# One hybrid decoder layer on one core: the first part's input loaded in one go, and the sample rows finished before the dense tiles' last norms

## The chip, the cores and the metric

One core of a Trainium2 chip runs the whole kernel. The metric is the device time of one execution in microseconds (us); lower is better. The core has a matrix engine (TensorE, PE in the profile, its weight loads PEld), a vector engine (VectorE, DVE), a scalar engine (ScalarE, ACT), GpSimd (POOL) and SyncE (SP), which here only issues transfers. Each engine takes its own instructions strictly in program order; they wait for each other by semaphores. [...]

## The reference

One layer of a decoder for a prompt of 1024 tokens and a sample of 8 x 4 tokens, all of width 1024 and in float32:

```python
h = rms_norm(x, norm_mix);  z = h @ w_in            # 28 column chunks of 128
A = dilated sliding-window attention (8 heads x 64) # q, k, v: chunks 0..11
B = gated linear recurrence (4 heads x 128)         # q, f, i, g: chunks 12..27
x += concat([rms_norm(A), gated B]) @ w_out
x += cross_attention(rms_norm(x), memory)           # 256 memory tokens
x += peer_ffn(rms_norm(x))                          # each token: 8 heads x 16 of 16384 experts
y = rms_norm(x, norm_final)
# peer_ffn, per token: e = chosen expert numbers, g = softmax of their scores
#   a = gelu(sum_d x[d] * peer_u[e, d]);   y = sum_e g * a * peer_v[e]
```

## The kernel before

The prompt is worked in three parts of tokens, `PARTS = ((0,1,2), (3,4,8), (5,6,7))`, in tiles of 128; "tile" 8 is the 32 sample rows, which ride along with the first part through the projection `z` and with the second from there on. Everything is float32 made of two fp32r halves (`hi`, `lo`), so each product is three matmuls (lines 201 to 203): weights hi times x hi, weights hi times x lo, weights lo times x hi, for each of eight blocks `c` of 128 input columns, in the order of `c`.

**The start.** `head()` of the first part loads the tokens twice: as rows (`in_x`, tiles tagged `P`, two buffers, then a Square with an accumulated sum on ScalarE, line 326) and transposed (`in_xT`, eight column blocks, tiles `ht`, two buffers). From the sums it makes 1/rms (line 210, on GpSimd), spreads it over the partitions by TensorE (line 217) into `bc`, and `norm_T` (lines 226 to 232) then takes each block: multiply with gain and `bc` (line 230, VectorE), copy to `hi` (line 169, ScalarE), difference to `lo` (line 170, VectorE). The first projection chunk can run its block `c` when `zhi` and `zlo` of it are there. Weights come as `raw` (two buffers), are split into `wz` (three buffers), used, and written to memory (`wd`) for the later parts. Before `head()` the program loads constants: `ident`, `par`, `bias_p`, `lmask`, `misc`, `iota`, `sum4`.

**The middle.** Attention, recurrence, cross attention and the choice of experts of the three parts are interleaved generators.

**The end.** Of the nine tiles, five (`DENSE`, tiles 0 to 4) are done by `dense()`: all 128 groups of 128 experts are streamed through TensorE (`a` = x times u, gelu, times gate, then `y`/`yr` = w times v); three tiles stay in PSUM (`y0`..`y5`), two are added to `ys` by VectorE from the one bank `yr`. `u` tiles have 5 buffers, `v` tiles 11. The other four tiles (8, 7, 6, 5, in this order) are done by `gather_tile()`: for each of up to 128 experts of a token GpSimd fetches one row per token (`row`, 7 buffers, line 1183), VectorE multiplies and sums (line 1190 for peer_u, line 1201 for peer_v, into `ha`). The two streams run side by side: TensorE works on dense, GpSimd and VectorE on the gather with VectorE's share of dense between. Behind each tile stands `final_norm` (lines 1144 to 1153): Square on ScalarE, a small VectorE step, a power on GpSimd (line 1149), the load of the final gain `gfin` spread over the rows (line 1151), a VectorE multiply, the store. The sample rows, whose gather tile was the first of the four and waits in memory as `accd`, are finished by `finish_sample` (lines 1207 to 1216): two matmuls sum four groups of rows, then `final_norm`.

The order on each engine is made by the framework's list scheduler, which follows a time line of its own; code that stands earlier comes first among what is ready. It also hands out the buffers of a tag. SP's transfers use eight completion slots in turn: a transfer is issued only after the one eight before it has landed.

Of the kernel before, what the change touches and what calls it, by code (L numbers as in the profile page):

```python
# [20 lines left out]
D = 1024  # L21
# [8 lines left out]
def col(p, n):  # L30
    return p[:, n : n + 1]
# [33 lines left out]
def _body(tc, nc, ctx, A, O):  # L65
# [43 lines left out]
    par = T(cst, [128, 64], F32, "par")  # L109
    SP.dma_start(par, A["par"])  # L110
    G_MIX, G_CR, G_FFN, G_MEM, BETA, GNB, LBL = 0, 8, 16, 24, 32, 36, 40
    bias_p = T(wk, [128, 1024], F32, "biasp")
    SP.dma_start(bias_p, A["bias_p"])
    lmask = T(wk, [128, 8, 128], U8, "lmask")
    lmf = T(pk, [128, 8, 128], F32, "tw", 2)
    SP.dma_start(lmf, A["lmask"])
    V.tensor_copy(lmask, lmf)
    smask = T(cst, [32, 3, 32], U8, "smask")
    V.tensor_copy(smask, lmf[:32, :3, :32])
    misc = T(cst, [128, 64], F32, "misc")  # L120
    SP.dma_start(misc, A["misc"])
    DM_A, DM_X, SEL, BEX = misc[:, 0:8], misc[:, 8:12], misc[:, 12:28], misc[0:32, 28:36]
# [175 lines left out]
    def part(pi):  # L298
# [21 lines left out]
        def head():  # L320
            ss = T(wk, [128, 4], F32, "n_ss")
            V.memset(ss, 1.0)
            for j, (t, o, rows) in enumerate(zt):
                m = T(wk, [128, 1024], F32, "P", 2)
                SP.dma_start(m[:rows], A["x"][t * 128 : t * 128 + rows, :])
                S.activation(m[:rows], m[:rows], AF.Square, accum_out=col(ss, j)[:rows])
            bc = bcast(rstd_of(ss[:, : len(zt)], len(zt), D), zt, "m", HB)

            def x_of(c):
                t = T(wk, [128, WZ], F32, "ht", HTB)[:, :WZP]  # L330
                load_xT(t, c, WZP)
                return t

            h.extend(norm_T(x_of, WZP, G_MIX, bc, hi_lo(TAGS["Z"]), True))

# [704 lines left out]
    def dense(dv, dn, dps):  # L1040
# [66 lines left out]
        for i in range(128):  # L1107
            hist.append(nxt)
            nxt = []
            ahead = hidden(i + 1, nxt) if i < 127 else iter(())  # L1110
            kept = [(t, dh) for t in range(KEEP) for dh in range(2)]
            sums = [(t, dh) for t in range(KEEP, NDT) if i % GRP == t % GRP or i == 127 for dh in range(2)]

            def keep(n):
                for t, dh in kept[:n]:
                    product(yp[2 * t + dh], t, dh, hist[i:], i == 0, i == 127)
                del kept[:n]

            next(ahead, None)
            keep(KEEP - 1)  # L1120
            next(ahead, None)
            for t, dh in sums:
                keep(1)
                ds = slice(dh * 512, (dh + 1) * 512)
                o = T(dps, [128, 512], F32, "yr", 1 if KEEP > 2 else 2)
                product(o, t, dh, hist[done[t] :], True, True)
                V.tensor_tensor(ys[t - KEEP][:, ds], ys[t - KEEP][:, ds], o, op=ALU.add)  # L1127
                done[t] = done[t] + dh * (i + 1 - done[t])
            keep(len(kept))
            next(ahead, None)  # L1130
            yield
        for t in range(NDT):
            if t < KEEP:
                acc = T(dn, [128, D], F32, "u", 5)
                SP.dma_start(acc, x2d[DENSE[t]])
                for dh in range(2):
                    ds = slice(dh * 512, (dh + 1) * 512)
                    V.tensor_tensor(acc[:, ds], acc[:, ds], yp[2 * t + dh], op=ALU.add)
            else:
                acc = ys[t - KEEP]  # L1140
            final_norm(acc, 128, O["y_prompt"][DENSE[t] * 128 : (DENSE[t] + 1) * 128, :],
                       lambda: T(dn, [128, D], F32, "u", 5), dn)

    def final_norm(acc, rows, out, row, p):
        st = T(p, [128, 4], F32, "fst", 2)
        jk = row()
        S.activation(jk[:rows], acc, AF.Square, accum_out=col(st, 0)[:rows])
        V.tensor_scalar(col(st, 1)[:rows], col(st, 0)[:rows], 1.0 / D, EPS, op0=ALU.mult, op1=ALU.add)
        G.tensor_tensor(col(st, 2)[:rows], col(st, 1)[:rows], mhalf[:rows, 0:1], op=ALU.pow)
        gfin = row()  # L1150
        SP.dma_start(gfin[:rows], A["gfin"].to_broadcast([rows, 1024]))
        V.scalar_tensor_tensor(acc, acc, col(st, 2)[:rows], gfin[:rows], op0=ALU.mult, op1=ALU.mult)
        SP.dma_start(out, acc)

# [7 lines left out]
            return T(more, [128, D], F32, "row", MR)  # L1162
        return T(gat, [128, D], F32, "row", 2)

    def gather_tile(t):
        smp = t == 8
        nj = 32 if smp else 128
        ix = T(gat, [128, 128], U32, "ix", 2)[:, :nj]
# [33 lines left out]
        if smp:  # L1202
            SP.dma_start(accd, acc)
        else:
            final_norm(acc, 128, O["y_prompt"][t * 128 : (t + 1) * 128, :], g_row, gat)

    def finish_sample(dn, dps):
        row = lambda: T(dn, [128, D], F32, "u", 5)
        acc = row()
        SP.dma_start(acc, accd)  # L1210
# [1 line left out]
        for n in range(2):  # L1212
            p = T(dps, [128, 512], F32, "yr", 1)
            PE.matmul(p[:32], lhsT=sum4, rhs=acc[:, n * 512 : (n + 1) * 512], start=True, stop=True)
            V.tensor_copy(fin[:32, n * 512 : (n + 1) * 512], p[:32])
        final_norm(fin[:32], 32, O["y_sample"], row, dn)

    def run(weights, *gens):
        gens = [(iter(g), n) for g, n in zip(gens, weights)]
# [20 lines left out]
    def ahead(q):  # L1240
        q.head()
        q.first_a()

    ahead(p[0])
    p[0].first_h()
    run(W0, p[0].middle(lambda: ahead(p[1])), memory_kv())
    p[1].first_h()
# [6 lines left out]
    with tc.tile_pool(name="dn", bufs=1, reuse_waits="tile") as dn, \  # L1254
# [4 lines left out]
            f()  # L1259
        late.close()  # L1260
        more = ctx.enter_context(tc.tile_pool(name="more", bufs=1, side="right", reuse_waits="tile"))
        for _ in work:
            pass
        for t in [t for part in PARTS for t in sorted(part, reverse=True) if t not in DENSE]:
            gather_tile(t)
        finish_sample(dn, dps)


def _consts():
# [100 lines left out]
```

## Time and profile before

| | |
|---|---|
| median of 3 runs | 3629.08 us (3626.5 to 3631.28) |
| profiled execution: time, span | 3627.68 us, 3625.8 us |
| busy: PE, DVE, ACT, POOL | 3373.7, 2634.7, 1220.6, 1112.5 us |
| transfers | 1007.82 MB, 278 GB/s over the span |

The span is the time between the first and the last recorded instruction; the execution's own time is 1.88 us longer. Busy times of engines overlap, so they do not add up to the span. A busy matrix engine is not one at its peak, since its matmuls are pipelined.

### The profile page before, as it was taken

The page shows a single profiled execution, that of the slowest core. Times are in us where ns is not written, and L with a number is a line of the kernel's source. Part 1 is how long each engine was busy: PE and PEld are TensorE (multiplying, and loading weights), DVE is VectorE, ACT ScalarE, POOL GpSimd, SP SyncE. Part 2 cuts the span into 40 slices and gives each one's busy share as a digit, 9 for nine tenths or more (in the row PEclk, how much of TensorE's full clock was granted, in tenths as well). Part 3 has the DMA queues.
Part 4 walks back from the last instruction along what each step waited for, and adds up shares of the span by engine and source line. Part 5 has one row for each costly group of instructions (what it writes and reads, how often), then busy time and mean ns, then how long its engine had stood idle before and what let it go on. Part 6 is the DMA issues. An engine that isn't in the chain of part 4 may idle for free.

```text
span 3625.8 us, 52725 instructions
## 1 busy us (share of the span) xinstructions
PE 3373.7 (93%) x19343; PEld 2912.4 (80%) x19343; DVE 2634.7 (73%) x5868; ACT 1220.6 (34%) x2282; POOL 1112.5 (31%) x871
## 2 busy tenths in 40 slices
PE   5999999999999889887799999999999999999994
PEld 4886776677887788777788998999888898988893
DVE  4443333243885687897888878988888898888997
ACT  4544344344434443431242222222222222222221
POOL 0000000000000000021316644656566565565555
PEclk9999999999999999898999999999999999999997
DMA  7667777656655485499659988999999999999998
GB/s 243 230 226 248 239 247 240 202 181 220 210 192 201 179 293 209 150 338 344 229 169 348 341 291 286 364 351 337 340 335 351 345 333 342 337 343 332 329 328 296
DMA packets 408514, 1007.82 MB, mean 278 GB/s; under 512 B 43968, under 2 KB 168896, under 8 KB 406848
## 3 DMA queue, kind: packets, MB, share of 16 engines
q1 hardware_dynamic: 288448, 568.20, 45.6%
q0 software_dynamic: 119808, 436.26, 33.0%
q8 instruction: 152, 2.49, 0.3%
q14 instruction: 106, 0.87, 0.1%
HBM read 866.01 MB, written 138.31 MB: 277 GB/s over the span
## 4 chain that ended last, share of the span: by engine, by line
PE 71%; DVE 10%; DMA 9%; issue 4%; ACT 3%; POOL 1%; SPq 1%; POOLq 0%; DVEq 0%; ACTq 0%
PE a L201 7%; PE a L203 7%; PE a L202 7%; PE y L1098 4%; PE y L1099 4%; PE y L1100 4%; PE z L201 4%; PE z L202 3%; PE z L203 3%; PE yr L1098 3%; PE yr L1099 2%; PE yr L1100 2%; PE y L201 2%; PE y L202 2%; PE y L203 2%
## 5 line engine op out<-in xcount | busy, mean ns | idle before, releaser
L1183 POOL DMA_INDIRECT row<-in_peer_u,ix x416 | 534.6, 1285 | 635.9 <-DVE dots L1190 347.6
L1183 POOL DMA_INDIRECT row<-in_peer_v,ix x416 | 543.1, 1306 | 412.1 <-DVE ha L1201 266.5
L201 PE MATMUL a<-xh,u 128*128 128x320 f32 x2048 | 636.8, 311 | 21.2 <-ACT w L1088 18.0
L203 PE MATMUL a<-xh,u 128*128 128x320 f32 x2048 | 634.5, 310 | 0.7 <-DVE u L170 0.7
L202 PE MATMUL a<-xl,u 128*128 128x320 f32 x2048 | 634.1, 310 | 0.0
L1201 DVE SCALAR_TENSOR_TENSOR ha<-row,dots,ha 128x1024 f32<-128x1024 f32 x416 | 533.0, 1281 | 22.2 <-DMA row<-in_peer_v,ix 17.8
L1190 DVE CUSTOM_DVE_ANT_0 row<-row,ha 128x1024 f32<-128x1024 f32 x416 | 497.9, 1221 | 39.5 <-DMA row<-in_peer_u,ix 39.5
L210 POOL TENSOR_TENSOR rs_r<-rs_m,mhalf 128x3 f32<-128x3 f32 (+2 forms) x25 | 23.4, 944 | 1369.7 <-DVE rs_m L208 1250.2
L1088 ACT ACTIVATE w<-a 128x320 f32<-128x320 f32 x256 | 111.6, 436 | 937.3 <-PE a L203 917.1
L201 PEld LDWEIGHTS a<-xh,u 128*128 128x128 f32 x2048 | 385.6, 188 | 40.5 <-ACT w L1088 25.8
L202 PEld LDWEIGHTS a<-xl,u 128*128 128x128 f32 x2048 | 385.7, 188 | 8.8
L203 PEld LDWEIGHTS a<-xh,u 128*128 128x128 f32 x2048 | 385.5, 188 | 2.8 <-DVE u L170 1.0
L201 PE MATMUL z<-zhi,wz 128*128 128x384 f32 (+2 forms) x928 | 330.4, 356 | 43.0 <-DMA wz<-wd_w_pq 16.2
L202 PE MATMUL z<-zlo,wz 128*128 128x384 f32 (+2 forms) x928 | 316.8, 341 | 3.4 <-DVE zlo L170 1.9
L203 PE MATMUL z<-zhi,wz 128*128 128x384 f32 (+2 forms) x928 | 314.0, 338 | 0.0
L1099 PE MATMUL y<-v,w 128*128 128x512 f32 x768 | 294.6, 392 | 0.0
L1098 PE MATMUL y<-v,w 128*128 128x512 f32 x768 | 269.6, 393 | 12.6 <-ACT v L169 11.2
L1100 PE MATMUL y<-v,w 128*128 128x512 f32 x768 | 264.5, 391 | 1.3 <-DVE w L170 1.2
L201 PEld LDWEIGHTS z<-zhi,wz 128*128 128x128 f32 x928 | 181.0, 195 | 87.3 <-issue 21.7
L1098 PE MATMUL yr<-v,w 128*128 128x512 f32 x512 | 201.8, 394 | 13.5 <-DVE ys L1127 11.7
L169 ACT CAST w<-w 128x320 fp32r<-128x320 f32 x256 | 117.8, 460 | 259.0 <-DVE w L1090 258.5
L1100 PE MATMUL yr<-v,w 128*128 128x512 f32 x512 | 199.9, 390 | 0.7 <-DVE w L170 0.7
(470 smaller groups left out, 6685.2 us busy)
## 6 DMA issues: line engine op xcount, KB each, us to landing
u<-in_uT SPq DMA_DIRECT2D x128, 512.0 KB, 7.0
v<-in_peer_v SPq DMA_DIRECT2D x128, 512.0 KB, 7.6
wz<-wd_w_in SPq DMA_DIRECT2D x112, 512.0 KB, 4.3
gt<-gtall SPq DMA_DIRECT2D x124, 320.0 KB, 10.8
wd_w_in<-wz SPq DMA_DIRECT2D x56, 512.0 KB, 3.2
gtall<-sg SPq DMA_DIRECT2D x34, 512.0 KB, 4.1
wd_w_pq<-wt SPq DMA_DIRECT2D x32, 512.0 KB, 3.1
wt<-wd_w_pq SPq DMA_DIRECT2D x32, 512.0 KB, 4.5
```

What stands on the lines that cost most here:

```text
L169: S.copy(hi, src)
L201: PE.matmul(out, lhsT=whi, rhs=xhi[:, c, sl], start=c == 0, stop=False)
L202: PE.matmul(out, lhsT=whi, rhs=xlo[:, c, sl], start=False, stop=False)
L203: ins = PE.matmul(out, lhsT=wlo, rhs=xhi[:, c, sl], start=False, stop=c == kc - 1)
L210: G.tensor_tensor(r, m, mhalf[:, :n], op=ALU.pow)
L1088: S.activation(ga[:, lo:hi], pa, AF.Gelu)
L1098: PE.matmul(o, lhsT=wh[:, sl], rhs=vh[:, ds], start=start and q == 0, stop=False)
L1099: PE.matmul(o, lhsT=wh[:, sl], rhs=vl[:, ds], start=False, stop=False)
L1100: PE.matmul(o, lhsT=wl[:, sl], rhs=vh[:, ds], start=False, stop=stop and q == len(ws) - 1)
L1183: G.indirect_dma_start(out=row, out_offset=None, in_=tab, in_offset=bass.IndirectOffsetOnAxis(ap=col(ix, j), axis=0))
L1190: V.tensor_tensor_reduce(row, row, hn, 1.0, 0.0, op0=ALU.mult, op1=ALU.add, accum_out=col(dots, j))
L1201: V.scalar_tensor_tensor(acc, row, col(dots, j), acc, op0=ALU.mult, op1=ALU.add)
```

## The change

Four edits.

1. The loads of `bias_p` and `lmask` and the two casts made of the latter move from the top of the program to behind the first part's `head()` and first three projection chunks.
2. In the first part, row tiles 2 and 3 of `in_x` go into the idle buffers `thi` and `tlo` in place of waiting for `P`, and the transposed blocks 2 to 7 are loaded in pairs into the idle buffers `vals`, `kT` and `vn`; blocks 0 and 1 stay in `ht`.
3. At the end, the three residual tiles of the PSUM tiles and `gfin` are loaded once into four `v` buffers, behind the last expert group; `final_norm` takes this `gfin` for the dense tiles, the sample and the last gathered tile.
4. The code of the first gathered tile (8) and of `finish_sample` moves ahead of the dense tiles' final norms.

```diff
-    bias_p = T(wk, [128, 1024], F32, "biasp")
-    SP.dma_start(bias_p, A["bias_p"])
-    ... lmask, lmf, smask
@@ head()
-                m = T(wk, [128, 1024], F32, "P", 2)
+                m = T(wk, [128, 1024], F32, *(("P", 2) if pi or j < 2 else (("thi", "tlo")[j - 2],)))
                 SP.dma_start(m[:rows], A["x"][t * 128 : t * 128 + rows, :])
                 S.activation(m[:rows], m[:rows], AF.Square, accum_out=col(ss, j)[:rows])
+            early = {}
+            if not pi:
+                for c in range(2, 8, 2):
+                    tag = {2: "vals", 4: "kT", 6: "vn"}[c]
+                    w = {"vals": [128, VALS], "kT": [128, 1024], "vn": [128, 1024]}[tag]
+                    two = T(pk if tag == "vals" else wk, w, F32, tag)[:, : 2 * WZP].rearrange("p (c t) -> p c t", c=2)
+                    load_xT(two, slice(c, c + 2), WZP)
+                    early[c], early[c + 1] = two[:, 0], two[:, 1]
             bc = bcast(rstd_of(ss[:, : len(zt)], len(zt), D), zt, "m", HB)
 
             def x_of(c):
-                t = T(wk, [128, WZ], F32, "ht", HTB)[:, :WZP]
-                load_xT(t, c, WZP)
-                return t
+                if pi or c < 2:
+                    t = T(wk, [128, WZ], F32, "ht", HTB)[:, :WZP]
+                    load_xT(t, c, WZP)
+                    return t
+                return early[c]
@@ dense(), behind the loop over the 128 groups
+        accs = []
+        for t in range(KEEP):
+            accs.append(T(dv, [128, D], F32, "v", 11))
+            SP.dma_start(accs[t], x2d[DENSE[t]])
+        gfin = T(dv, [128, D], F32, "v", 11)
+        SP.dma_start(gfin, A["gfin"].to_broadcast([128, 1024]))
+        yield gfin
         for t in range(NDT):
             if t < KEEP:
-                acc = T(dn, [128, D], F32, "u", 5)
-                SP.dma_start(acc, x2d[DENSE[t]])
+                acc = accs[t]
@@ final_norm(acc, rows, out, row, p, gfin=None)
-        gfin = row()
-        SP.dma_start(gfin[:rows], A["gfin"].to_broadcast([rows, 1024]))
+        if gfin is None:
+            gfin = row()
+            SP.dma_start(gfin[:rows], A["gfin"].to_broadcast([rows, 1024]))
@@ the program
     ahead(p[0])
+    bias_p = ... ; lmask = ... ; smask = ...
     p[0].first_h()
...
+        gfin = None
+        while gfin is None:
+            gfin = next(work)
+        rest = [t for part in PARTS for t in sorted(part, reverse=True) if t not in DENSE]
+        gather_tile(rest[0])
+        finish_sample(dn, dps, gfin)
         for _ in work:
             pass
-        for t in [t for part in PARTS for t in sorted(part, reverse=True) if t not in DENSE]:
-            gather_tile(t)
-        finish_sample(dn, dps)
+        for t in rest[1:]:
+            gather_tile(t, gfin if t == rest[-1] else None)
```

The instructions stand in another order in three places that matter below. Line numbers of the changed program differ a little: its lines 162, 222 and 1192 are lines 170, 230 and 1183 of the kernel before.

On VectorE at the start, before (`ht` are the transposed blocks, `zlo` the low halves of the normalised ones, `wz` the weights):

```order
L230 SCALAR_TENSOR_TENSOR ht_203<-ht_203,par_80,bc_194 128x416
L230 SCALAR_TENSOR_TENSOR ht_209<-ht_209,par_80,bc_194 128x416
L170 TENSOR_TENSOR zlo_202<-ht_203,zhi_201 128x416
L170 TENSOR_TENSOR zlo_202<-ht_209,zhi_201 128x416
L170 TENSOR_TENSOR wz_294<-raw_295,wz_294 128x512
L230 SCALAR_TENSOR_TENSOR ht_215<-ht_215,par_80,bc_194 128x416
```

The same place in the changed program:

```order
L222 SCALAR_TENSOR_TENSOR ht_204<-ht_204,par_80,bc_195 128x416
L222 SCALAR_TENSOR_TENSOR vals_182<-vals_182,par_80,bc_195 128x416 x2
L222 SCALAR_TENSOR_TENSOR kT_185<-kT_185,par_80,bc_195 128x416 x2
L222 SCALAR_TENSOR_TENSOR vn_188<-vn_188,par_80,bc_195 128x416 x2
L222 SCALAR_TENSOR_TENSOR ht_210<-ht_210,par_80,bc_195 128x416
L162 TENSOR_TENSOR zlo_203<-ht_204,zhi_202 128x416
L162 TENSOR_TENSOR wz_235<-raw_236,wz_235 128x512
L162 TENSOR_TENSOR zlo_203<-vals_182,zhi_202 128x416 x2
L162 TENSOR_TENSOR wz_242<-raw_243,wz_242 128x512
L162 TENSOR_TENSOR zlo_203<-kT_185,zhi_202 128x416 x2
L162 TENSOR_TENSOR zlo_203<-vn_188,zhi_202 128x416
L1259 CAST lmask_362<-tw_363 128x1024
```

Behind these come the small second cast, the other low half of `vn` and, last, that of `ht_210`. All eight multiplies now stand ahead of the first low half, and block 1 (`ht_210`), which TensorE wants second, comes last.

On GpSimd at the end, before: the last fetches (line 1183) and the powers of the final norms (line 1149; the one of 32 rows is the sample's):

```order
L1183 DMA row_32190<-in_peer_v,ix_31417 128x1024
L1183 DMA row_32193<-in_peer_v,ix_31417 128x1024
L1149 TENSOR_TENSOR fst_29606<-fst_29606,mhalf_100 128x1
L1149 TENSOR_TENSOR fst_29615<-fst_29615,mhalf_100 128x1
L1149 TENSOR_TENSOR fst_32196<-fst_32196,mhalf_100 128x1
L1149 TENSOR_TENSOR fst_29624<-fst_29624,mhalf_100 128x1
L1149 TENSOR_TENSOR fst_32214<-fst_32214,mhalf_100 32x1
```

The same place in the changed program:

```order
L1192 DMA row_32180<-in_peer_v,ix_31416 128x1024
L1157 TENSOR_TENSOR fst_29792<-fst_29792,mhalf_92 32x1
L1192 DMA row_32183<-in_peer_v,ix_31416 128x1024
L1157 TENSOR_TENSOR fst_29801<-fst_29801,mhalf_92 128x1
L1192 DMA row_32186<-in_peer_v,ix_31416 128x1024
L1192 DMA row_32189<-in_peer_v,ix_31416 128x1024
L1157 TENSOR_TENSOR fst_29810<-fst_29810,mhalf_92 128x1
L1192 DMA row_32192<-in_peer_v,ix_31416 128x1024
L1157 TENSOR_TENSOR fst_29819<-fst_29819,mhalf_92 128x1
L1157 TENSOR_TENSOR fst_29826<-fst_29826,mhalf_92 128x1
L1157 TENSOR_TENSOR fst_29833<-fst_29833,mhalf_92 128x1
L1157 TENSOR_TENSOR fst_32195<-fst_32195,mhalf_92 128x1
```

The sample's power moved from last to ahead of the last four fetches, and the last gathered tile's (`fst_32195`) is now the last of all. On VectorE the six other final multiplies now stand ahead of the last four accumulations; before, two did.

On SP at the start of the dense stage, before (`wz` the expert-choice weights of the third part, `xh` and `xl` the dense stage's input):

```order
L186 DMA wz_15218<-wd_w_pq_0_1472_6867 128x1024
L1047 DMA xh_15700<-h3x_65_163 128x1280
L1047 DMA xl_15701<-h3x_66_164 128x1280
L1047 DMA xh_15700<-h3x_65_163 128x1280
L186 DMA wz_15220<-wd_w_pq_1_1475_6874 128x1024
L1047 DMA xl_15701<-h3x_66_164 128x1280
L1047 DMA xh_15700<-h3x_65_163 128x1280
```

The same place in the changed program (weights of the same place have a number smaller by 3):

```order
L178 DMA wz_15263<-wd_w_pq_0_1480_6922 128x1024
L1049 DMA xh_15691<-h3x_61_155 128x1280
L1049 DMA xl_15692<-h3x_62_156 128x1280
L1049 DMA xh_15691<-h3x_61_155 128x1280
L1049 DMA xl_15692<-h3x_62_156 128x1280
L1049 DMA xh_15691<-h3x_61_155 128x1280
L178 DMA wz_15265<-wd_w_pq_1_1483_6929 128x1024
```

Five input loads now stand between two weight loads in place of three, and the weights are two loads further ahead when they begin. Nobody wrote this: the scheduler's choices shift all along the middle of the program.

## Rows read from the trace of the kernel before

**Rows 1.** The page's busy tenths of PE in 40 equal slices of the span

```profile
PE   5999999999999889887799999999999999999994
```

**Rows 2.** Busy by stretch (window, length, busy us per engine, PEclk, DMA share, GB/s)

```profile
0.00:48.00 48.00, 12.84 (x30) 8.08 (x30) 17.68 (x45) 17.18 (x31) 1.88 (x6) 1.00 0.75 250
...
1640.00:1900.00 260.00, 217.41 (x1179) 197.72 (x1179) 216.49 (x768) 77.68 (x113) 60.75 (x44) 0.93 0.71 247
...
2200.00:2500.00 300.00, 296.50 (x1660) 268.64 (x1659) 268.24 (x302) 79.06 (x129) 178.31 (x138) 1.00 0.95 342
...
3560.00:3604.00 44.00, 14.59 (x65) 10.95 (x64) 39.32 (x42) 5.90 (x11) 26.95 (x22) 0.76 0.91 330
```

**Rows 3.** Timeline of the start (start, duration, engine, line, operation, idle before it)

```profile
6.73 0.69 DVE L117 CAST lmask<-tw 128x1024 uint8<-128x1024 f32 x1 [2.16 <-DMA tw<-in_lmask]
...
14.15 0.66 SPq L325 DMA_DIRECT2D P<-in_x  x1
...
21.14 1.05 ACT L326 ACTIVATE P<-P 32x1024 f32<-32x1024 f32 x1 [1.44 <-DMA P<-in_x]
...
22.32 0.17 DVE L208 TENSOR_SCALAR rs_m<-n_ss 128x4 f32<-128x4 f32 x1 [6.29 <-ACT P L326]
...
25.37 1.21 DVE L230 SCALAR_TENSOR_TENSOR ht<-ht,par,bc 128x416 f32<-128x416 f32 x2 [2.75 <-ACT bc L220]
...
26.63 1.16 DVE L170 TENSOR_TENSOR zlo<-ht,zhi 128x416 fp32r<-128x416 f32 x2
...
28.88 0.69 DVE L170 TENSOR_TENSOR wz<-raw,wz 128x512 fp32r<-128x512 f32 x1 [1.10 <-ACT wz L169]
...
48.35 0.71 PE L201 MATMUL z<-zhi,wz 128*128 128x416 f32 x1 [1.11 <-ACT zs L352]
...
53.37 0.48 PE L203 MATMUL z<-zhi,wz 128*128 128x416 f32 x1
53.70 0.35 PE L201 MATMUL z<-zhi,wz 128*128 128x416 f32 x1
53.88 0.35 PE L202 MATMUL z<-zlo,wz 128*128 128x416 f32 x1
```

**Rows 4.** The chain that ended last, from 27 to 44 us: start, us, what

```profile
27.62 3.20 DMA ht<-in_xT
...
34.14 2.62 DMA ht<-in_xT
...
40.85 2.97 DMA ht<-in_xT
```

**Rows 5.** Busy by stretch, from 13 to 26 us (columns as in group 2)

```profile
13.00:26.00 13.00, 1.76 (x6) 0.97 (x6) 2.27 (x7) 6.65 (x13) 1.69 (x2) 1.00 1.01 352
```

**Rows 6.** Timeline of the end (columns as in group 3)

```profile
3562.95 1.28 DVE L1201 SCALAR_TENSOR_TENSOR ha<-row,dots,ha 128x1024 f32<-128x1024 f32 x1
...
3564.15 1.28 DVE L1138 TENSOR_TENSOR u<-u,y 128x512 f32<-128x512 f32 x2
...
3602.17 1.28 DVE L1201 SCALAR_TENSOR_TENSOR ha<-row,dots,ha 128x1024 f32<-128x1024 f32 x1 [1.46 <-DMA row<-in_peer_v,ix]
3603.49 1.06 ACT L1147 ACTIVATE row<-ha 128x1024 f32<-128x1024 f32 x1 [9.76 <-DVE ha L1201]
...
3604.90 1.54 POOL L1149 TENSOR_TENSOR fst<-fst,mhalf 128x1 f32<-128x1 f32 x1 [9.09 <-DVE fst L1148]
...
3613.74 1.89 PE L1214 MATMUL yr<-u,sum 128*32 128x512 f32 x2 [34.88 <-DMA u<-accd]
...
3622.45 0.32 SPq L1153 DMA_DIRECT2D out_y_sample<-u  x1
```

**Rows 7.** Transfers issued from 3540 us on: count, KB each, median us to landing

```profile
u<-in_gfin SPq DMA_DIRECT2D x5, 512.0 KB, 8.5
...
row<-in_peer_v,ix POOLq DMA_INDIRECT x29, 6.3
```

**Rows 8.** PE's waits from 1640 to 1900 us: us in total, times, longest

```profile
PE z L201 <- DMA wz<-wd_w_pq: 16.2, 6, 6.0
```

More of the change, by code (lines that the diff above doesn't have):

```diff
@@ L111, in _body @@
     G_MIX, G_CR, G_FFN, G_MEM, BETA, GNB, LBL = 0, 8, 16, 24, 32, 36, 40
-    bias_p = T(wk, [128, 1024], F32, "biasp")
-    SP.dma_start(bias_p, A["bias_p"])
[L114 to L119, printed above, removed]
     misc = T(cst, [128, 64], F32, "misc")
@@ L1141, in dense, with final_norm @@
             final_norm(acc, 128, O["y_prompt"][DENSE[t] * 128 : (DENSE[t] + 1) * 128, :],
-                       lambda: T(dn, [128, D], F32, "u", 5), dn)
-    def final_norm(acc, rows, out, row, p):
+                       lambda: T(dn, [128, D], F32, "u", 5), dn, gfin)
+    def final_norm(acc, rows, out, row, p, gfin=None):
         st = T(p, [128, 4], F32, "fst", 2)
@@ L1163, in g_row, with gather_tile @@
         return T(gat, [128, D], F32, "row", 2)
-    def gather_tile(t):
+    def gather_tile(t, gfin=None):
         smp = t == 8
@@ L1204, in gather_tile, with finish_sample @@
         else:
-            final_norm(acc, 128, O["y_prompt"][t * 128 : (t + 1) * 128, :], g_row, gat)
-    def finish_sample(dn, dps):
+            final_norm(acc, 128, O["y_prompt"][t * 128 : (t + 1) * 128, :], g_row, gat, gfin)
+    def finish_sample(dn, dps, gfin):
         row = lambda: T(dn, [128, D], F32, "u", 5)
@@ L1215, in finish_sample @@
             V.tensor_copy(fin[:32, n * 512 : (n + 1) * 512], p[:32])
-        final_norm(fin[:32], 32, O["y_sample"], row, dn)
+        final_norm(fin[:32], 32, O["y_sample"], row, dn, gfin)
     def run(weights, *gens):
@@ L1244, in _body @@
     ahead(p[0])
+    bias_p = T(wk, [128, 1024], F32, "biasp")
+    SP.dma_start(bias_p, A["bias_p"])
+    lmask = T(wk, [128, 8, 128], U8, "lmask")
+    lmf = T(pk, [128, 8, 128], F32, "tw", 2)
+    SP.dma_start(lmf, A["lmask"])
+    V.tensor_copy(lmask, lmf)
+    smask = T(cst, [32, 3, 32], U8, "smask")
+    V.tensor_copy(smask, lmf[:32, :3, :32])
     p[0].first_h()
```

## The prediction

> **What bounds the kernel now.** I read first the page's slices [rows 1]: TensorE is busy nine tenths or more nearly everywhere; the reader should see the exceptions, the first slice (5), some between 1180 and 1810 us, and the last (4). Then busy times by stretch [rows 2]. In the dense stage (2200 to 2500 us) TensorE is busy 296.5 of 300 us, VectorE 268: TensorE sets the pace, and work that the change puts on VectorE or takes off it there moves nothing. In the first 48 us TensorE works 12.8; from 3560 to 3604 us 14.6 of 44, while VectorE works 39.3. So the change touches the two ends, where TensorE waits.
>
> Then the timeline of the start [rows 3]. The fourth row tile is issued at 14.15 us, since its buffer had to be given back first, and used at 21.14; the sums are ready at 22.3, the first multiply runs at 25.4, and the second projection chunk starts only at 48.35. In between TensorE waits three times for two more transposed blocks, 3.20, 2.62 and 2.97 us [rows 4]. Last the end [rows 6]: the last fetched row is accumulated at 3602.2 to 3603.45; behind it come the last gathered tile's norm, three dense tiles' norms that were still open, and, all by itself, the sample: two matmuls at 3613.74 and later, a store issued at 3622.45, the end of the span at 3625.8. That is 22.35 us behind the last row.
>
> **The start, step by step.** The four row tiles and the constants ahead of them are 1.9 MB. The stretch from 13 to 26 us shows what the transfer engines give when they are full: 352 GB/s at a share of 1.01 [rows 5]. 1.9 MB take 5.4 us of it; SP issues five constants first (about 3 us, an estimate from issues of under 0.7 us as at 14.15), and I allow 2 us for the way: the last tile is there at about 10, its Square done at 12. That is 10.3 us earlier than 22.3. From the sums to the first multiply it is 3.05 us as before: 15.0.
>
> Now the order takes something back. All eight multiplies run first, 8 x 0.605 = 4.8 us, then eight low halves, 8 x 0.58 = 4.6, with two weight halves of 0.69 and the mask's casts (0.69 and a small one, 0.9 together) between [rows 3]: 15.0 + 4.8 + 4.6 + 1.4 + 0.9 = 26.7. Block 1 is last of these and TensorE needs it second, so TensorE runs three matmuls, and from the fifth on waits until 26.7. Then 20 matmuls remain; at the spacing of this stretch, about 0.34 us (53.37 to 53.70), that is 6.8 us, then 1.3 to empty the bank (1.11 before, and the last matmul's own length): the second chunk starts at 34.8 in place of 48.35, **13.5 us** earlier. The transposed blocks, 1.7 MB more, take 4.8 us at 352 GB/s and land by 15 to 16; the first weights stand behind all of this on SP and land near 17, ten us ahead of 26.7. So their delay, and that of `bias_p` and `lmask`, is hidden by VectorE's list; past 27 it would cost what it is late.
>
> [...] Between the bounds of nothing and of both chunks' remaining matmuls (35 x 0.15 = 5.3) I take the second chunk's first 15, which were slow: 15 x 0.15 = **2.3 us**. [...] Against it: the memory tokens' norm, which ran in TensorE's gaps before, now runs beside the next chunks. I charge **2**, between nothing and the 5 us by which 15 to 20 operations of 0.4 to 0.6 would delay a chunk. Start: 13.5 + 2.3 - 2 = **13.8 us**, bounds 8 (sums only 7 us earlier, the wait from 14.15 to 21.14; no clock; 2.2 charged) and 17.
>
> [...]
>
> **The end.** From the accumulation at 3562.95 on, the changed VectorE order has 20 accumulations, before 22: two more rows are taken earlier, beside dense, where VectorE has 32 us of 300 free [rows 2]. Steps are 1.20 us for a 1024-wide pass and 0.6 for 512 (3562.95 to 3564.15; two adds in 1.28) [rows 6]. After: 20 x 1.2 = 24, six adds 3.6, four `yr` adds 2.6, six final multiplies 7.2, two sample copies 1.2, small ones 0.9: 39.5, so 3602.5 if it never waits. The same count before is 26.4 + 3.6 + 2.6 + 2.4 + 0.9 = 35.9, 3598.9, and it was 3603.45: 4.5 us of waiting. I take 4 for the changed order, **3606.5**: its new waits are for the sample's two matmuls (1.89 for two of four pieces, twice) and for powers on GpSimd, which stand between the last four fetches. What is queued behind each power is a fetch; seven row buffers and a landing of 6.3 us [rows 7] give it slack. Then the last norm: 1.45 us to the power, 1.54, a multiply of 1.2, an issue of 0.35, in all 4.6 [rows 6]. The store of the sample took 3.0 us from the end of its issue to the end of the span; one of 512 KB has 0.4 MB more, 1.1 us: 4.1. End: 3606.5 + 4.6 + 4.1 = 3615.2, **10.6 us** earlier than 3625.8. The sample, its 15.5 us from 3607 on, lies beside the fetches.
>
> `gfin` was loaded once for each norm, five of 512 KB from `u` alone [rows 7]; one load saves 2 MB before the last row, 6 us of the engines at 330 GB/s [rows 2]. Three stores that came behind now come ahead, 4.7 us. I count the two against each other. The early loads of residuals cost nothing: they wait for `v` buffers that are used last some 15 us before the adds. Bounds of the end: 14.2 with no wait at all, 4.6 with one more landing of 6 us ahead of the last row.
>
> **The middle.** The scheduler's order shifts from the start to the dense stage. TensorE is idle 43 us of 260 from 1640 on [rows 2], 16.2 of it for expert-choice weights [rows 8]; five input loads now stand between two of them, but the weights are two loads further ahead. I take 0, bounds 8 either way, half of that wait.
>
> **Sum.** 13.8 + 10.6 = 24.4. The profiled execution took 3627.7, so 3603.3; the median lies 1.4 above it: **3605**.
>
> **Rivals.** *The start's gain is given back* (chance 0.12): the weights' chain of load, split and store sets the pace behind the second chunk. For it speaks that few weights can be ahead (three buffers); against it that TensorE is busy nine tenths from the second slice on. Then only the end is left: 3629 - 11 = 3618. *The end's gain is halved or lost* (0.12): a power waits for the sample's sums and the last fetches behind it go out late. For it: GpSimd's new order, four fetches behind it. From about 6 us of delay on, 3611; at 10.6, 3615. *More than forecast* (0.10): sums at 10, the rise of the clock in the first chunk, no wait at the end, weights further ahead in the middle: 17 + 14, 3598 or less. *Slower* (0.05): in the new order the choice weights of the third part wait behind five loads of 655 KB; if this wait, 16.2 us now, holds up the whole choice of experts and with it the gather, three times over (+32), the time is 3637. It decides from 24 us of added wait on. *The change does nothing at either end* (0.03): the first rows still wait for the transfer engines and the end for the fetches, 3629.
>
> **How the numbers follow.** Forecast 0.58, own range 3598 to 3612. Two in ten are left out by 3593 to 3620: the corner of both high bounds (-31) with 8 gained in the middle lies below it, the slow and the idle case above. 0.2% (7 us) is about what a measurement here tells from no change. Faster is the forecast, the larger gain, and most of the first two rivals: 0.88. Same: 0.07. Slower: 0.05.
>
> **What would show it.** Right: the second chunk starts at 33 to 37 us; TensorE waits once, between its third and fifth matmul, for the low half of block 1; behind the last accumulation stands one norm, under 10 us to the end of the span; the sample's store leaves before it; one `gfin` load. Wrong: a start of the second chunk past 42; weights landing past 27; fetches going out more than 2 us late behind a power; a dense stage that starts less than 8 us earlier than before; any stretch of the middle longer by more than 8.

## The result, and the profile after

The changed kernel took 3597.57 us (median of four runs, 3583.46 to 3604.17) against 3630.18 (3626.5 to 3634.51): ratio 0.990, interval 0.988 to 0.992. Its profiled execution took 3604.17 us, 23.5 less than that of before; 24.4 less was forecast. The median fell by 32.6, a third more, to 0.4 us below the forecast's own range of 3598 to 3612 (but within 3593 to 3620). That the two profiles come so near to the forecast is in part luck: the one after is the slowest of its four runs, and what lies between the two ends differs by 8 us and more from one execution to the next (below). The two ends moved nearly as forecast; the experiments show that several reasons given for it were wrong.

The page's busy tenths of PE, and busy times by stretch (columns as in [rows 2]):

```profile
PE   7999999999999889787899999999999999999995
```

```profile
0.00:48.00 48.00, 23.85 (x95) 19.06 (x96) 20.95 (x58) 22.43 (x50) 1.91 (x6) 1.00 0.89 308
1640.00:1900.00 260.00, 220.22 (x1187) 201.19 (x1186) 213.96 (x723) 78.33 (x113) 65.83 (x51) 0.92 0.72 248
2200.00:2500.00 300.00, 298.81 (x1677) 271.79 (x1676) 274.77 (x312) 78.95 (x131) 188.03 (x142) 1.00 0.96 349
3540.00:3590.00 50.00, 23.72 (x113) 18.02 (x111) 45.17 (x52) 8.58 (x16) 33.07 (x26) 0.82 0.86 313
```

Beside [rows 1, 2] the first slice has 7 in place of 5, and TensorE works 11 us more in the first 48; the stretches between look alike. The timelines of the start, of VectorE, TensorE and ScalarE (columns as in [rows 3]):

```profile
12.81 0.17 DVE L200 TENSOR_SCALAR rs_m<-n_ss 128x4 f32<-128x4 f32 x1 [8.09 <-ACT tlo L318]
...
15.86 0.65 DVE L222 SCALAR_TENSOR_TENSOR ht<-ht,par,bc 128x416 f32<-128x416 f32 x1 [2.74 <-ACT bc L212]
...
25.84 0.57 DVE L162 TENSOR_TENSOR zlo<-ht,zhi 128x416 fp32r<-128x416 f32 x1
```

```profile
26.47 0.72 PE L194 MATMUL z<-zlo,wz 128*128 128x416 f32 x1 [3.81 <-DVE zlo L162]
...
31.49 0.55 PE L193 MATMUL z<-zhi,wz 128*128 128x416 f32 x1
31.84 0.40 PE L194 MATMUL z<-zlo,wz 128*128 128x416 f32 x1
32.07 0.35 PE L195 MATMUL z<-zhi,wz 128*128 128x416 f32 x1
32.26 0.35 PE L193 MATMUL z<-zhi,wz 128*128 128x416 f32 x1
...
33.80 0.46 PE L193 MATMUL z<-zhi,wz 128*128 128x416 f32 x1 [0.81 <-ACT zs L354]
34.09 0.35 PE L194 MATMUL z<-zlo,wz 128*128 128x416 f32 x1
```

```profile
32.53 0.62 ACT L161 CAST wz<-raw 128x512 fp32r<-128x512 f32 x1 [7.74 <-DMA raw<-in_w_in]
...
39.28 0.21 ACT L354 COPY zs<-z 128x32 f32<-128x32 f32 x1
```

The last line is the copy behind the second chunk; before, it stood at 56.39:

```profile
56.39 0.19 ACT L352 COPY zs<-z 128x32 f32<-128x32 f32 x1
```

The three waits of [rows 4] are one wait of 3.81 us for the low half of block 1, last in VectorE's list. The second chunk starts at 33.80 in place of 48.35. TensorE had run without a gap from 26.47, and its clock rose inside the first chunk, as the distance from one matmul to the next shows: 0.35 us until 31.84, then 0.19. (PEclk can't be read there: it says 1.00 for 26.5 to 31.5, while in the run `b1early` below the same distance, from 32 to 35, goes with 0.50.) One thing to watch: the second chunk's first weights were split at 32.53, only just ahead of their use. The end (columns as in [rows 6]):

```profile
3550.04 1.28 DVE L1210 SCALAR_TENSOR_TENSOR ha<-row,dots,ha 128x1024 f32<-128x1024 f32 x1
...
3573.92 0.34 SPq L1162 DMA_DIRECT2D out_y_sample<-u  x1
...
3579.59 1.28 DVE L1161 SCALAR_TENSOR_TENSOR v<-v,fst,v 128x1024 f32<-128x1024 f32 x1 [1.50 <-POOL fst L1157]
...
3589.74 5.24 DVE L1210 SCALAR_TENSOR_TENSOR ha<-row,dots,ha 128x1024 f32<-128x1024 f32 x4
...
3595.02 1.06 ACT L1155 ACTIVATE row<-ha 128x1024 f32<-128x1024 f32 x1 [9.90 <-DVE ha L1210]
```

The last row is accumulated at 3594.98; one norm stands behind it, and the span ends 6.8 us later at 3601.8, where it was 22.35 [rows 6]. The sample's store leaves at 3573.92. Of the transfers issued from 3540 us on, the gain's is one, where [rows 7] had five:

```profile
v<-in_gfin SPq DMA_DIRECT2D x1, 512.0 KB
```

### The profile page after: what moved, and what is told of

Read it like the earlier page. It is cut to its first block, busy times and chain, and to the rows that moved or that the text cites. A ratio compares the mean times of both kernels' runs of the same rounds, so it can differ in the third digit from the quotient of the medians.

```text
span 3601.8 us, 52661 instructions
## 1 busy us (share of the span) xinstructions
PE 3376.9 (94%) x19343; PEld 2917.0 (81%) x19343; DVE 2629.6 (73%) x5860; ACT 1222.5 (34%) x2289; POOL 1106.9 (31%) x871
## 3 DMA queue, kind: packets, MB, share of 16 engines
q1 hardware_dynamic: 287584, 565.45, 45.8%
## 4 chain that ended last, share of the span: by engine, by line
PE 73%; DMA 10%; DVE 8%; issue 4%; ACT 2%; POOL 1%; SPq 1%; POOLq 0%; ACTq 0%; DVEq 0%
PE a L193 7%; PE a L195 7%; PE a L194 7%; PE y L1100 4%; PE y L1101 4%; PE y L1102 4%; PE z L193 4%; PE z L194 3%; PE z L195 3%; PE yr L1100 3%; PE yr L1101 3%; PE yr L1102 3%; PE y L193 2%; PE y L194 2%; PE y L195 2%
## 5 line engine op out<-in xcount | busy, mean ns | idle before, releaser
L193 PE MATMUL z<-zhi,wz 128*128 128x384 f32 (+2 forms) x928 | 329.2, 355 | 34.6 <-DMA wz<-wd_w_pq 17.3
L1100 PE MATMUL yr<-v,w 128*128 128x512 f32 x512 | 202.4, 395 | 12.1 <-DVE ys L1129 10.6
```

The source lines that it names most:

```text
L193: PE.matmul(out, lhsT=whi, rhs=xhi[:, c, sl], start=c == 0, stop=False)
L1100: PE.matmul(o, lhsT=wh[:, sl], rhs=vh[:, ds], start=start and q == 0, stop=False)
```

## The experiments

Every run is measured against the kernel before on the same chip. The table has one profiled execution of each kernel: when the second chunk starts; from there to the start of the last gelu of the dense stage (the middle); from that gelu to the end of the last accumulation, and to the end of the span; how many rows are still to be accumulated behind the last gate multiply; then the median of all its runs, the ratio to before and its interval. Times are in us. Beside these sets of runs the kernel before had medians from 3628.67 to 3639.05, so kernels of different sets are compared by the ratio.

| kernel | 2nd chunk | middle | gelu to last row | to end | rows left | median | ratio |
|---|---|---|---|---|---|---|---|
| before | 48.35 | 3513.7 | 41.4 | 63.7 | 22 | 3630.18 | |
| changed | 33.80 | 3515.4 | 45.8 | 52.7 | 20 | 3597.57 | 0.990 (0.988 to 0.992) |
| again | 33.75 | 3507.5 | 45.8 | 52.6 | 20 | 3599.27 | 0.991 (0.9884 to 0.9936) |
| start | 32.91 | 3521.7 | 36.2 | 58.4 | 20 | 3607.78 | 0.9933 (0.9909 to 0.9958) |
| rows | 47.23 | 3524.4 | 36.1 | 59.4 | 20 | 3627.81 | 0.9987 (0.9969 to 1.0004) |
| pairs | 33.07 | 3506.6 | 45.8 | 52.6 | 20 | 3596.49 | 0.989 (0.9869 to 0.9912) |
| pairs_only | 40.62 | 3526.1 | 48.5 | 55.3 | 22 | 3614.65 | 0.9955 (0.9938 to 0.9972) |
| b1early | 32.13 | 3523.6 | 45.8 | 52.6 | 20 | 3599.97 | 0.9902 (0.9877 to 0.9928) |
| lean | 28.84 | 3530.2 | 48.5 | 55.3 | 22 | 3608.82 | 0.9936 (0.9915 to 0.9958) |
| res8 | 29.03 | 3520.7 | 45.8 | 52.6 | 20 | 3599.66 | 0.9889 (0.9868 to 0.9909) |
| end | 49.22 | 3519.0 | 48.5 | 55.8 | 22 | 3626.19 | 0.9987 (0.9972 to 1.0002) |
| no4 | 32.77 | 3521.4 | 43.2 | 51.1 | 20 | 3599.78 | 0.9911 (0.9889 to 0.9933) |
| no3 | 32.95 | 3529.1 | 33.4 | 60.5 | 20 | 3613.09 | 0.9952 (0.9933 to 0.9971) |
| best8 | 29.55 | 3514.6 | 43.2 | 51.0 | 20 | 3596.42 | 0.9896 (0.987 to 0.9921) |

**The changed kernel again** (no edit).

> The changed kernel once more, unaltered, for its own spread: its four runs lay 20.7 us apart (3583.5 to 3604.2), the four of the kernel before 8.0. If the spread belongs to the new order of the program, the runs lie over 12 us apart again, around 3598; if the one run of 3583 was an exception, they lie within 8 us of each other, between 3595 and 3606. A second profile shows which stretch of the program differs from the first one's when the span does.

Six runs from 3593.84 to 3607.69: the spread stays. But it isn't the new order's: 22 runs of the kernel before, beside the second set of experiments, lay between 3622.55 and 3645.26. The two profiles have the same first and last stretch to 0.1 us, and their middles differ by 7.9. Over the five profiles whose matmuls stand in one and the same order (the changed kernel, `again`, `start`, `no4`, `no3`) the middle spans 21.6 us. So a single profile tells the two ends of this program to tenths, and the middle to no better than 8 us, seen over the five to some 20.

**The start alone, and the end alone.** `start` has edits 1 and 2, `end` edits 3 and 4.

> Edits 1 and 2 alone (the start), the end as before. Theory: the two ends add up. The second chunk starts 14.5 us earlier, as in the changed kernel, some 2 us are given back later, and the end keeps its 22.35 us behind the last accumulation: 12 to 15 us less than before, 3616. Rival, the start's gain is given back further on, and more of the changed kernel's gain comes from the end and from the scheduler's shifts in the middle: within 5 us of before, 3626 to 3630. Second rival, the shifts in the middle help: over 20 us less.

> Edits 3 and 4 alone (the end), the start as before. Theory: the last accumulation comes some 3 to 4 us later against the dense stage's last weighted sums than before, and behind it stand 7 us in place of 22: 11 us less than before, 3619. Rival, the new order in the middle is what costs or gains: with the start as before the scheduler's order there is another, and the gain lies outside 6 to 16 us while the two distances at the end are those of the changed kernel.

Neither theory held as stated. The start alone gains 20.9 us in median (beside 3628.67), the size of its second rival, but not in the middle: to its 15.4 us comes an end that is 5.3 shorter, with old code there. The scheduler's order shifted with the start, two more rows are accumulated beside the dense stage, and the last fetches are hardly waited for. VectorE's waits at the end, of before from 3560 to 3605 and of `start` from 3552 to 3593 (line and releaser: us in total, times, longest):

```profile
DVE ha L1201 <- DMA row<-in_peer_v,ix: 3.3, 3, 1.5
DVE fst L1148 <- ACT row L1147: 1.2, 1, 1.2
```

```profile
DVE fst L1150 <- ACT row L1149: 1.2, 1, 1.2
DVE ha L1203 <- DMA row<-in_peer_v,ix: 0.5, 1, 0.5
```

The end alone is 7.9 us shorter in its own stretch, 63.7 to 55.8, with 22 rows left as before. Its order is that of before up to the last fifty instructions of VectorE, so the 5.3 us that its middle took longer are the spread just seen, and its interval (10 us faster to 1 slower) holds 7.9 as it holds nothing. On top of the start the two edits bring 8.5 us in median (`start` to `again`, measured beside the same runs of before; the intervals overlap).

**Which half of edit 2, and what edit 1 is worth.** `rows` is the kernel before with edit 1 and the row tiles' half; `pairs` is the changed kernel without that half:

```diff
-                m = T(wk, [128, 1024], F32, *(("P", 2) if pi or j < 2 else (("thi", "tlo")[j - 2],)))
+                m = T(wk, [128, 1024], F32, "P", 2)
```

`pairs_only` takes edit 1 back as well.

> Edit 1 and the half of edit 2 that moves row tiles 2 and 3 to idle buffers, on the kernel before: the transposed blocks still come one by one through two buffers, and the end is that of before. By the terms of the prediction the sums are 9.5 to 10.3 us earlier than at 22.3, and the three waits for transposed blocks (8.8 us) stay or grow: the second chunk starts at 38 to 41 us in place of 48.35, 7 to 10 us earlier, and the pairs are worth the other 5 to 7 of the 14.5. Rival: with the engines full (a share of 1.04 from 13 to 32 us in the changed kernel) the blocks that are issued one by one stand behind the bulk loads, and the second chunk starts past 43: nearly all of the start's gain is the pairs'. In time: 6 to 12 us less than before by the first, within 6 by the second.

> The changed kernel with the other half of edit 2 undone: row tiles 2 and 3 wait for their old buffers again, the transposed blocks stay in pairs in idle buffers. With the row tiles alone (the last experiment on the start) the second chunk's copy came at 55.54 us, 0.85 us earlier than before, though the sums were ready at 12.4: the waits for transposed blocks grew to 11 us in their place. Theory A, each half alone gains little, since the other's wait takes its place: the sums stay at 20 to 22 us, the second chunk's copy at 46 us or later. Theory B, the pairs carry the gain: the sums come at 16 to 20 (fewer bulk loads ahead of the last row tile), and with all blocks there VectorE's list of 10.6 us runs at once: the second chunk's copy at 41 to 45 us, 11 to 15 us earlier than at 56.39 before, and the time 3 to 6 us above the changed kernel's.

> The changed kernel with edit 1 undone as well as the row tiles' half of edit 2: bias and mask are loaded and cast at the top again, and of the start only the pairs remain. The last experiment on the start (pairs with edit 1) had the sums at 16.5 us, 3.7 later than the changed kernel, and its second chunk at 33.07, 0.7 earlier, since its VectorE list held two weight splits fewer and block 1 second. Theory: what counts is when VectorE can begin its low halves; with bias and mask ahead the sums come at 19 to 22.3 us, the first multiply at 22 to 25.4, the low halves 4.6 us after it, and TensorE runs without a gap from 28 to 31: the second chunk starts at 35 to 38.5 us, 10 to 13 us earlier than before, and the time is 2 to 5 us above the changed kernel's. Rival: the sums, the mask's casts or the weights come later still, and the second chunk starts past 41: then edit 1 is worth more than half of the start.

With the row tiles early and the blocks one by one the sums are ready at 12.36, and the second chunk starts at 47.23, 1.1 us earlier than before: the rival, past 43 (its last clause, that nearly all of the gain is then the pairs', `pairs_only` corrects). The chain of `rows` shows why (columns as in [rows 4]):

```profile
13.32 9.42 DMA sg<-in_kc
22.75 6.45 DMA ht<-in_xT
...
32.52 2.69 DMA ht<-in_xT
...
39.30 3.38 DMA ht<-in_xT
```

The buffer for the third block was free at 18.4, when the low halves of the first two ended; its two loads were issued at 22.12 and 22.75. The one eight transfers ahead of the latter had to land first, a load of 256 KB (`sg`) that took 9.42 us among the bulk loads, and then the block's own second load, 16 KB of sample columns, took 6.45, with the transfer engines at a share of 1.05 (22 to 30 us). Nearly all the time won in front was lost there. With the pairs and old row buffers (`pairs`, theory B, and better than its 41 us: the second copy falls at 38.55), the sums come at 16.48, 3.7 us later than in the changed kernel, and still the second chunk starts at 33.07, 0.7 earlier. VectorE's list is shorter (the weights were split before the first multiply) and has block 1 in its place; the fifth matmul no longer waits, and TensorE runs without a gap from 25.42, the changed kernel from 26.47:

```profile
24.63 0.23 DVE L1261 CAST smask<-tw 32x96 uint8<-32x96 f32 x1
24.80 1.07 DVE L162 TENSOR_TENSOR zlo<-ht,zhi 128x416 fp32r<-128x416 f32 x2
```

```profile
25.42 0.72 PE L194 MATMUL z<-zlo,wz 128*128 128x416 f32 x1 [3.90 <-DVE zlo L162]
```

`pairs_only` fell between its two expectations: sums at 20.54, second chunk at 40.62, 7.7 us earlier than before. So of 15.3 us the pairs alone bring 7.7, edit 1 beside them 7.6, the row tiles nothing. But not all of the 7.6 are the two loads. The sums are 4.1 us later than in `pairs`, and besides, the new order puts a matmul of the memory tokens' norm into the first chunk, where TensorE waits for a power on GpSimd that took 4.49 us (from 28.75):

```profile
33.30 0.69 PE L217 MATMUL x<-ident,rs_r 128*128 128x128 f32 x2 [2.67 <-POOL rs_r L210]
```

Some 3 us are this shift of the order. In median and ratio `pairs` is as fast as the changed kernel, and `pairs_only` 17 to 18 us slower: 7.6 of them are the start and 2.7 two rows more at the end; the rest is in its middle and not explained.

**What binds the second chunk now.** `b1early` has blocks 0 and 1 in the first pair; `lean` and `res8` besides make loads wait for matmuls.

```diff
-                for c in range(2, 8, 2):
-                    tag = {2: "vals", 4: "kT", 6: "vn"}[c]
+                for c in range(0, 6, 2):
+                    tag = {0: "vals", 2: "kT", 4: "vn"}[c]
...
-                if pi or c < 2:
+                if pi or c > 5:
... (lean: bias_p, lmask behind the last matmul of chunk 0, res of chunk 2; res8: res alone, of chunk 8)
+                behind(SP.dma_start(xr[:, :, :NP], A["xT"][:, :, c0 : c0 + NP]), 8)
```

> The changed kernel, but the pairs of transposed blocks are 0 and 1, 2 and 3, 4 and 5, and blocks 6 and 7 take the two ht buffers, so that block 1 is no longer the last low half on VectorE. Theory A: VectorE's list sets the start of the second chunk; TensorE then loses its wait of 3.8 us ahead of the fifth matmul, follows the low halves and ends the first chunk about 4 us earlier: the second chunk starts at 29 to 30 us, the time is 3 to 4 us less than that of the changed kernel. Theory B: the second chunk's weights are nearly the bound as well (their first half was split at 32.53 us, 8.76 us after its load was issued, with the transfer engines at a share of 1.04): the second chunk starts no earlier than 33, and the time is within 1.5 us of the changed kernel's.

> The order of blocks as in the experiment with blocks 0 and 1 in the first pair, and besides three loads that the start doesn't need wait for TensorE: the attention bias and the mask (1 MB) for the last matmul of the first chunk, the residual of the first part (1.5 MB) for that of the third. So 2.5 MB fewer stand ahead of the second chunk's weights, and the mask's casts leave VectorE's list. If the transfer engines bind the second chunk (the first copy of the first chunk came 5.6 us earlier in that experiment, 27.92 for 33.56 us, but that of the second at 38.99 for 39.28), its weights come some 6 us earlier, and the copy of the second chunk falls at 32 to 35 us; the time is 4 to 6 us less than that experiment's 3600. If something else binds it, the second copy stays past 37.5 us. If the later bias and mask hold up the first attention, or the start's gain is given back in the chain of weights, the second copy comes early and the time stays within 2 us.

> The order of blocks with 0 and 1 in the first pair, and only the residual's load (1.5 MB) waits, for the last matmul of the ninth chunk; bias and mask stand where the changed kernel has them. If the transfer engines bind the second chunk, its first weights come 1.5 MB or about 4 us earlier than in the experiment with that order of blocks (split at 31.46 us there): TensorE's wait of 4.8 us ahead of the second chunk shrinks under 1.5 and its clock doesn't fall again, so the second copy falls at 33.5 to 35.5 us in place of 38.99. In time 3 to 5 us less than 3600, if the start's gain is kept; if the loss in the experiment that delayed bias, mask and residual (3609) came from the residual, over 3605 again; if it came from bias and mask, at or under 3600.

In `b1early` TensorE follows the low halves, the clock rises inside the first chunk (from 0.35 us between matmuls to 0.19, at 24.94), and that chunk ends 5.6 us earlier. Then TensorE waits for weights, 4.76 us, and its clock is low again, 0.35 us between matmuls until 35.10:

```profile
27.02 0.35 PE L195 MATMUL z<-zhi,wz 128*128 128x416 f32 x1
32.13 0.71 PE L193 MATMUL z<-zhi,wz 128*128 128x416 f32 x1 [4.76 <-ACT wz L161]
32.64 0.55 PE L194 MATMUL z<-zlo,wz 128*128 128x416 f32 x1
...
35.33 0.35 PE L193 MATMUL z<-zhi,wz 128*128 128x416 f32 x1
```

Theory B holds in the main (the start is at 32.13 and not past 33), with the clock on top: 1.7 us of earlier start, of which 1.4 go into nine slow matmuls; the copy behind the second chunk came 0.3 earlier than the changed kernel's. With 1.5 MB out of the way (`res8`) the chunk starts at 29.03 and its copy falls at 34.51, as expected, 4.8 us ahead of the changed kernel's. The time can't show it: 3599.66, its ratio 0.9889 and the changed kernel's 0.990 and 0.991 with intervals that overlap. `lean` starts as early, has its second copy at 36.30, between the bounds given, and is 9 us slower than `b1early`, which none of its expectations had. Two more rows at its end are 2.7 of them. For the rest there is a likely cause, not tested apart: bias and mask come late, the memory tokens' rows, which share two buffers with the mask, are issued at 30.65 and 38.84 in place of 15.57 and 29.01, and from 60 to 91 us TensorE works 27.73 of 31 us in place of the changed kernel's 30.76.

**Which edit makes the end.** `no4` puts the sample's code back behind the dense norms, `no3` lets each norm load its own gain and residual.

> The changed kernel with edit 4 undone: the residuals and the gain are loaded once and early, but the code of the sample and of tile 8 stands behind the dense norms again. Up to the last fifty instructions of each engine its order is the changed kernel's, so what differs is the stretch from the last gelu to the end: 52.7 us in the changed kernel, 63.7 before. Theory A, the one early gain and the early residuals carry the end's gain: without them a dense norm waited for a buffer and for a load of 512 KB (8.5 us to land); the six multiplies find their powers done, since no power stands one accumulation ahead of its multiply, and the sample ends beside the last rows or at most 2 us behind: 50 to 54 us, the time within 3 us of the changed kernel's. Theory B, the sample's chain behind the last row was the tail (12 us from its first matmul at 3613.74 to the end before) and the new order of the code carries the gain: 58 us or more, the time 5 to 11 us above the changed kernel's.

> The changed kernel with edit 3 undone: the sample and tile 8 still stand ahead of the dense norms, but each norm loads its own gain into one of the five u buffers, and the residuals go there as well. From the last gelu to the end, by theory A: the dense norms queue for u buffers behind the sample, their multiplies (1.2 us each) and loads (8.5 us to land) come behind the last row: 60 us or more in place of 52.7, the time 7 us or more above the changed kernel's. By theory B (the order of the code carries the gain): 52 to 55 us, within 3 us.

Theory A, both times. Without edit 4 the stretch is 51.1 us, 1.6 shorter than with it; without edit 3 it is 60.5, no better than the old end's 58.4 and 59.4 with as many rows left. VectorE's waits in the changed kernel, 3547 to 3596, and in `no4`, 3552 to 3606:

```profile
DVE v L1161 <- POOL fst L1157: 2.4, 3, 1.5
DVE ys L1161 <- POOL fst L1157: 0.9, 2, 0.4
...
DVE u L1161 <- POOL fst L1157: 0.5, 1, 0.5
```

```profile
DVE u L1161 <- POOL fst L1157: 0.8, 1, 0.8
DVE ha L1161 <- POOL fst L1157: 0.7, 1, 0.7
DVE ys L1161 <- POOL fst L1157: 0.5, 1, 0.5
DVE v L1161 <- POOL fst L1157: 0.5, 1, 0.5
```

With edit 4 the multiplies of the five dense tiles and of the sample stand one accumulation behind their power each and wait 3.7 us in all. Without it these six wait 1.7, of which 0.8 (the first row, the sample's) falls behind the last row, where two norms stand then, 7.8 us in place of 6.8. (`ha`, the last gathered tile's, waits 0.7 behind the last row in both.) In median `no3` lies 15.5 us above the changed kernel; 7.8 of that are this stretch, the rest is in its middle, the second longest of the table, and can't be told from the spread. What `no3` waits for behind its last row are four loads of the gain, 8.7 us together; the first and the last of them:

```profile
3603.15 1.29 DVE L1156 SCALAR_TENSOR_TENSOR u<-u,fst,u 128x1024 f32<-128x1024 f32 x1 [3.08 <-DMA u<-in_gfin]
...
3616.41 1.28 DVE L1156 SCALAR_TENSOR_TENSOR ys<-ys,fst,u 128x1024 f32<-128x1024 f32 x1 [3.77 <-DMA u<-in_gfin]
```

Whether the one gain would do without the early residuals was not tried.

**All that looked good together**: `best8` is `res8` without edit 4.

> The same as the last one, with edit 4 undone as well (the sample's code behind the dense norms, which took 51.1 us from the last gelu to the end in place of 52.7). Theory: both gains add to the changed kernel's, 4 to 6 us less than it: 3593 to 3596. Rival: the start's 4 us are given back within the first 300 us, and 1 to 2 us are within what runs differ by: 3597 to 3600, no version better than the changed kernel that a measurement can tell.

3596.42, between the two, and by its ratio of 0.9896 no better than the rest: the rival's conclusion. Nothing here beats the changed kernel by more than its runs differ; whether the 4.8 us at the start and the 1.6 at the end are kept or given back stays open.

## Why the prediction was right, and where it wasn't

- *Start, 13.5 us*: 14.55. *Clock, 2.3*: with it the copy behind the second chunk is 17.1 us earlier (56.39 to 39.28), so 2.6; the last four matmuls of the first chunk were fast already, as the rival of a larger gain had it. No run shows the 2.3 itself: that 15 matmuls would come 0.15 us closer was the author's estimate, from 0.33 and 0.18 us in [rows 3]. What the runs show is that the second chunk's first 15 distances took 5.35 us before (48.35 to 53.70) and 2.94 in the changed kernel (33.80 to 36.74), 2.4 less; what makes the clock rise they don't show. The 2 us for the way are near what one load of before took, `par` with 32 KB: 1.9 from issue to landing. The low half of block 1 came at 25.84 (forecast as the end of the list, 26.7), the first multiply at 15.86 (15.0).
- The path was right, step by step. What failed is the weight of "that is 10.3 us earlier than 22.3" in the 13.5. The sums came early (12.81), but early sums alone gained 1.1 us (`rows`), and beside the pairs sums 3.7 later cost nothing (`pairs`), since VectorE's list was shorter there and had block 1 in its place. With that order mended the early sums do bring the first chunk's copy 4.9 us ahead of that of `pairs` (27.92 and 32.83, `b1early`), and then the second chunk waits for weights. What counted is that all eight blocks are there when VectorE begins, and edit 1. That was costed only as a delay hidden elsewhere; beside the pairs it is worth 7.6 us, some 3 of them by the scheduler's order. That the waits grow back behind bulk loads was seen for the weights alone.
- "Weights land near 17" was right for the first chunk. The second chunk's were not costed: they were split at 32.53 and would have cost any further gain at once (`b1early`).
- *Loads of single blocks*: where [rows 4] had waits of 3.20, 2.62 and 2.97 us, the waits that stayed in `rows`, counted from the issue of each block's second load of 16 KB, were 6.45, 2.69 and 3.38 us. The transfer engines' share was 1.05 at the first, 0.40 and 0.55 at the others (22 to 30, 30 to 36, 36 to 43 us). So the waits were near those of before where the engines had room, and the first about twice as long, where they were full.
- *End, 10.6 us*: 11.0 (63.7 to 52.7). The last accumulation lies 4.4 us later against the gelu, 3.05 were forecast; VectorE's waits for powers, 3.74 there, were forecast as 4 in all. Behind it stand 6.8 us; 8.7 were forecast, since the power took 0.54 us in place of 1.54 and the store's way to the end of the span 3.2 in place of 4.1. (By the sum's own figures its upper bound is 14.6, not 14.2.) But the term was given to edits 3 and 4. Two rows fewer are worth 2.7 us (55.3 to 52.6, new end) to 5 (63.7 to 59, old end, with its waits for fetches), and belong to the shifted order; edit 3 brings the rest; edit 4 costs 1.6.
- *Middle, 0 within 8*: the profiled middle took 1.7 us longer, the second profile's 6.2 less. The charge of 2 for the memory tokens' norm can't be told from this; in `pairs_only`, with a matmul of that norm inside the first chunk, it was some 3. That the median gained 9 us more than the profile is within the middle's spread and not explained further.
- The rivals: the start's gain was kept; no fetch went out so late that VectorE waited for its row; the choice weights held nothing up (TensorE waits 17.3 us for them in place of 16.2, and the dense stage starts at 1723.35 in place of 1736.08). More than forecast (0.10, 3598 or less) is where the median of the first four runs lies, and nearly that of the ten of both sets, 3598.3; of its reasons the runs show only the clock's rise in the first chunk (0.35 us between matmuls until 31.84, then 0.19).

## What to carry to other kernels

Where two loads wait for buffers in one full queue, freeing the earlier alone can move its time into the later (`rows`: a second chunk 1.1 us earlier, with a share of 1.05), while freeing the later alone can bring the whole gain (`pairs`: 15.3). Before an edit is credited with a gain, ask which single wait ends last with and without it; here one half of edit 2 and edit 4 ride along for nothing. Where a scheduler reorders everything, compare stretches between fixed points of two profiles of the same program first, to learn what a stretch's time is worth.

## What was not expected of the hardware

The middle's spread is in good part TensorE's clock. The same 22 matmuls, in the changed kernel and in its second profile (columns as in [rows 2]):

```profile
866.00:875.00 9.00, 9.00 (x22) 5.53 (x22) 2.47 (x8) 3.07 (x5) 0.00 (x0) 0.50 0.20 66
```

```profile
868.30:873.10 4.80, 4.80 (x22) 3.10 (x22) 2.56 (x8) 2.51 (x5) 0.00 (x0) 1.00 0.23 68
```

TensorE counts as wholly busy in both; granted are 0.50 and 1.00, and the same work takes 9.00 us and 4.80. In both profiles short matmuls of attention and sample (128x128, 128x4) stood in the few us ahead of it, so these alone don't decide it. Nothing was late there, and no edit touched it. What lowers the clock in one execution and not in the other no run shows. In the dense stage a part of the spread is weights that come late, a wait of 2.58 us at 2878.93 in the first profile that the second doesn't have:

```profile
2878.93 1.65 PE L1100 MATMUL y<-v,w 128*128 128x512 f32 x3 [2.58 <-ACT v L161]
```

With the slow matmuls behind it the first profile loses 4.3 us there (2875.96 to 2882.08, in the second 2873.11 to 2874.93). The two places together are 8.5 us, about what the two middles differ by in all (7.9).
